# Twenty of 32 gated-conv projection tiles as ten seven-product pairs behind the SSD

## The chip, the cores and the metric

The kernel runs on one core of a Trainium2 chip. TensorE (PE) multiplies, VectorE (DVE), ScalarE (ACT) and GpSimd (POOL) work on tiles, SyncE (SP) issues the loads and stores. The metric is the device time of one execution in microseconds; less is better.

## The reference

Two layers of an encoder, 1024 tokens of width 1024, in float32. The change lies in the first, even layer: one input projection feeds a bidirectional Mamba-2 SSD (16 heads in 4 groups, chunks of 128 tokens) and a short gated convolution; both outputs go through one output projection.

```python
proj = x @ w_in
z, xbc, dt_raw, sc_bg, sc_cg, sc_h, sc_gate = _split(proj, EVEN_SIZES)
...
y_a = _rms_norm(y_a.reshape(b, S, SSD_INNER).astype(x.dtype) * jax.nn.silu(z), norm_g)
y_b = sc_bg * _depthwise_conv(sc_cg * sc_h, sc_conv_w, (1, 1)) * jax.nn.silu(sc_gate)
return jnp.concatenate([y_a, y_b], axis=-1) @ w_out
```

The four parts of the gated convolution (sc_bg, sc_cg, sc_h, sc_gate) are 1024 wide each: 32 tiles of 128 columns, which the kernel names `("br", q, j)`, q = 0 to 3 for the part and j = 0 to 7 for the tile. The second layer (latent attention and pooling) isn't touched.

## The kernel before

Each float32 operand is split into a high and a low half in the matmul's type (a cast on ScalarE gives the high one, a subtraction on VectorE or GpSimd the low one), and a product is three matmuls: high by high, high by low, low by high. A projection tile of 128 columns and 1024 tokens is eight steps (one for each 128 of the depth) of `mm6`, six matmuls of 512 columns; its PSUM tile is called `gps` in the traces, its weights come from `wraw` as `whi` and `wlo`, through the class `Weights`, which loads and splits them in the order in which the tiles are used.

`main_plan` writes the order of the even layer as a list of steps, and a queue of tile steps (`fm`) is pulled into it as filler. For each SSD group g it has two phases:

- p2, for each of eight chunks: the z tile (`op_z`, 24 matmuls of 256 columns, `zps`), the transposes of x and B (`xps`), the state products (`op_p2s`, `sps`). Then `op_p2b` runs the backward recursion over the chunks' states `hin`, on GpSimd (`hm`) and VectorE in turn.
- p3, for each of eight chunks: `op_p3f` makes the decay matrix: it loads rows `E` and `tb`, ScalarE takes their relu and `Dm`, VectorE their maximum, ScalarE the exp, VectorE multiplies by `Dm` and by the C-B product (`cbp`), and the result is split into `Mh` and `Ml`. `op_p3x` splits `hin` into `hh`, `hl` and x into `xs`. `op_p3b` multiplies them (`yo` from hh and hl, `yd` from Mh, Ml and xs), adds up in `ta` on GpSimd and VectorE, gates with z on GpSimd (`yg`), squares on ScalarE (`ta,ssq`) and stores the row to memory (`yad`).

The plan puts FB = 6 steps of filler ahead of p2, FC = 4 ahead of p3 and F3 = 7 into each p3 chunk. The filler is the 32 br tiles in the order of j; ahead of them go the X tiles of the next group (before p3) and its B and C tiles (behind p3). Behind the SSD, `op_ya` transposes the gated rows for the output projection (`yat`, `yas`, `ahi`, `alo`), with the last br tiles between; `ops` are the output projection's matmuls. A scheduler then orders each engine's instructions; every engine runs its own in that order.

Of the kernel before, what the change touches and what calls it, by code (L numbers as in the profile page):

```python
# [18 lines left out]
P = 128  # L19
# [44 lines left out]
F2, F3, FB, FT, FC = 0, 7, 6, 4, 4  # L64
ROPE_AT = (2, 2)
L1_ORDER = "t0 l2 t1 l3 t2 l4 t3 l5 m0 l6 m1 l7".split()
YB_AT = (0, 1, 3, 4, 6, 7, 9, 10)
X_AT = (10, 11, 12, 13)
WOB, WOI, WOG, PI, NV, LA = 2, 3, 1, 1, 0, 2
T4B, T2B, CVB, RAWB = 1, 10, 3, 2  # L70


def main_plan():
    ops = []
    queue = []

    def tile_steps(key):
        return [("fm", key, kk) for kk in range(KD)]

# [12 lines left out]
    pull(8)  # L92
    ops.append(("dt",))
    pull(len(queue))
    for j in range(8):
        for q in BR_ORDER:
            queue += tile_steps(("br", q, j))
    for g in range(G):
        ops.append(("z0", g))
        pull(FB)  # L100
        for c in range(NB):
            ops.append(("p2", g, c))
            ops.append(("z", g, c))
# [17 lines left out]
        if g + 1 < G:  # L121
            to_front([("B", g + 1), ("C", g + 1)])
            while any(s[1][0] in ("B", "C", "X") for s in queue):
                pull(1)
    ops.append(("end",))
    for c in range(NB):
        pull(FT)
        ops.append(("ya", c))
    pull(len(queue))
    return ops  # L130

# [16 lines left out]
def weight_index():  # L148
    idx = {}
    for key in weight_seq():  # L150
        idx.setdefault(key, len(idx))
# [73 lines left out]
class Weights:  # L225
    def __init__(self, k, pool, ahead=1):
        self.k, self.pool, self.ahead = k, pool, ahead
        self.seq, self.idx = weight_seq(), weight_index()
        self.loaded = self.done = self.used = 0
        self.raw, self.out = {}, {}  # L230

    def load(self, upto):
        while self.loaded < min(upto, len(self.seq)):
# [6 lines left out]
    def split(self, upto):  # L240
        nc = self.k.nc
        while self.done < min(upto, len(self.seq)):
# [9 lines left out]
            self.load(i + 2)  # L252

# [219 lines left out]
def layer0_main(k):  # L473
# [6 lines left out]
    sctx = ExitStack()  # L480
    k.dts_pool = sctx.enter_context(tc.tile_pool(name="dts", bufs=1))
    cvp = sctx.enter_context(tc.tile_pool(name="cvp", bufs=1))
# [4 lines left out]
    xhi = [view(big(k, f"xhi{h}"), KD) for h in range(2)]  # L487
    xlo = [view(big(k, f"xlo{h}"), KD) for h in range(2)]
# [3 lines left out]
    for kk in range(KD):  # L492
        raw = dtp.tile([P, 2, HALF], F32, name="xraw", tag="xraw", bufs=4)
# [5 lines left out]
        for h in range(2):  # L499
            split(nc, xhi[h][:, kk, :], xlo[h][:, kk, :], raw[:, h, :], V)  # L500
# [24 lines left out]
    def t4(name):  # L525
        return tp.tile([P, S], F32, name=name, tag="t4", bufs=T4B)
# [29 lines left out]

    def fm_finish(key, ps):
# [8 lines left out]
        elif kd in ("B", "C"):  # L566
# [6 lines left out]
            for h in range(2):  # L573
                sl = slice(HALF * h, HALF * h + HALF)
                v = conv_half(ps, 8 + 4 * q + g, st["xfm"][:, 2, sl] if q == 0 else None, h)
                split(nc, st["bc"][:, 2 * q, sl], st["bc"][:, 2 * q + 1, sl], v, V)
        else:
# [5 lines left out]
            elif q == 2:  # L583
                u = br["u"]
                V.tensor_tensor(out=u, in0=ps, in1=u, op=ALU.mult)
                w = lambda i: k.vec[:, V_SCW + 3 * j + i:V_SCW + 3 * j + i + 1]
                br["a"] = []
                for h in range(2):
                    acc = tp.tile([P, 512], F32, name="bra", tag="bra", bufs=2)
                    A.mul(out=acc, in_=u[:, hs[h]], mul=w(1))  # L590
                    for i, sh in ((0, -1), (2, 1)):
                        a0 = 1 if h == 0 and sh < 0 else 0
                        a1 = HALF - 1 if h == 1 and sh > 0 else HALF
                        lo = HALF * h + sh
                        V.scalar_tensor_tensor(out=acc[:, a0:a1], in0=u[:, lo + a0:lo + a1], scalar=w(i), in1=acc[:, a0:a1], op0=ALU.mult, op1=ALU.add)
                    br["a"].append(acc)
# [14 lines left out]
    def op_fm(key, kk):  # L611
# [4 lines left out]
        mm6(nc, halves(ps), wh[:, kk, :], wl[:, kk, :], [t[:, kk, :] for t in xhi], [t[:, kk, :] for t in xlo], kk == 0, kk == KD - 1)  # L616
# [11 lines left out]
    def op_z(g, c):  # L628
# [3 lines left out]
        for kk in range(KD):  # L632
            wh, wl = st["zw"][kk // 4]
            mm3(nc, ps, xhi[h][:, kk, o:o + P], xlo[h][:, kk, o:o + P], view(wh, 4)[:, kk % 4, :], view(wl, 4)[:, kk % 4, :], kk == 0, kk == KD - 1)
# [131 lines left out]
    def op_end():  # L766
# [6 lines left out]
        k.ahi = [view(big(k, f"ahi{h}"), KD) for h in range(2)]  # L773
        k.alo = [view(big(k, f"alo{h}"), KD) for h in range(2)]

    def op_ya(c):
        h, o = c // 4, (c % 4) * P
        for q in range(2):
            y = t2("yab")
            nc.sync.dma_start(out=y, in_=k.yad[c, :, HALF * q:HALF * q + HALF])  # L780
            V.tensor_scalar(out=y, in0=y, scalar1=k.rinv[:, c:c + 1], scalar2=None, op0=ALU.mult)
            ps = k.pb.tile([P, 512], F32, name="yat", tag="pb")
            for f in range(4):
                PE.transpose(out=ps[:, P * f:P * f + P], in_=y[:, P * f:P * f + P], identity=k.ident)
            t = cv("yas")
            V.tensor_tensor(out=view(t, 4), in0=view(ps, 4), in1=bc_last(k.vec[:, V_NG + 4 * q:V_NG + 4 * q + 4], P), op=ALU.mult)
            split(nc, k.ahi[h][:, 4 * q:4 * q + 4, o:o + P], k.alo[h][:, 4 * q:4 * q + 4, o:o + P], view(t, 4), V)

    table = {"fm": op_fm, "z0": op_z0, "z": op_z, "p2": op_p2, "p2s": op_p2s, "p2b": op_p2b, "p3f": op_p3f, "p3x": op_p3x, "p3b": op_p3b, "dt": op_dt, "rope": lambda: rope_tables(k, t2), "end": op_end, "ya": op_ya}
    for op in main_plan():  # L790
        table[op[0]](*op[1:])
    sctx.close()
# [25 lines left out]
def outproj0(k):  # L818
# [40 lines left out]
    for h in range(2):  # L859
# [529 lines left out]
```

## Time and profile before

| | us |
|---|---|
| median of 3 runs | 1444.57 (1444.01 to 1447.03) |
| profiled execution | 1445.73 |
| its span, first to last instruction | 1444.0 |
| PE busy | 1416.2 (98%) |
| DVE, ACT, POOL busy | 921.9, 749.1, 480.5 |
| granted TensorE clock, mean | 0.997 |

The SSD with its filler runs from about 65 to 729 us of the span, the output projection of the even layer follows, and the odd layer comes behind it. Busy time is the sum of an engine's instructions; the length of a matmul's row contains time in which the next one already runs, so the distance between starts is the price of one. A pair of starts of the same kind, say two `Mh`, shows the time that a chunk takes.

### The profile page before, as it was taken

To read this page: it belongs to the slowest core of one execution; us is meant where nothing else is said; L and a number is where in the kernel's file an instruction comes from. 1 tells how busy PE (TensorE), PEld (TensorE's weight loads), DVE (VectorE), ACT (ScalarE), POOL (GpSimd) and SP (SyncE) were. 2 spreads that over 40 slices of the span, in tenths; PEclk is the share of its full clock that TensorE was granted. 3 is DMA by queue.
4 is the path that set the end of the run, shared out by engine and by line. 5 is a ranking of instruction groups with operands and counts; after the bars stand their busy time and mean duration, and the time that the engine had idled before them with its cause. 6 is when DMAs were issued, how large, how long until landed. Compare 5 with 4: busy or idle time off the path is not lost.

```text
span 1444.0 us, 20351 instructions
## 1 busy us (share of the span) xinstructions
PE 1416.2 (98%) x7454; PEld 1208.9 (84%) x7454; DVE 921.9 (64%) x1608; ACT 749.1 (52%) x1567; POOL 480.5 (33%) x479
## 2 busy tenths in 40 slices
PE   7999999999999999999989999999999999999997
PEld 5898888888898888988868888898888888988886
DVE  5837666666687665647683543733326888888485
ACT  5447654576447773566443332522224788888510
POOL 0032541435322452445400160612320355556210
PEclk9999999999999999999999999999999999999999
DMA  6102331323203321133525556201110000001232
GB/s 219 48 30 89 113 84 38 93 78 111 70 30 103 112 86 52 59 110 95 164 99 175 204 175 200 89 31 59 44 37 1 1 1 1 1 30 59 89 117 88
DMA packets 46483, 118.57 MB, mean 82 GB/s; under 512 B 5808, under 2 KB 10288, under 8 KB 46384
## 3 DMA queue, kind: packets, MB, share of 16 engines
q1 hardware_dynamic: 46384, 117.27, 25.5%
q8 instruction: 59, 0.97, 0.3%
q14 instruction: 40, 0.33, 0.1%
HBM read 100.34 MB, written 16.91 MB: 81 GB/s over the span
## 4 chain that ended last, share of the span: by engine, by line
PE 44%; DVE 4%; issue 1%; ACT 1%; DMA 0%; POOL 0%; DVEq 0%; ACTq 0%; POOLq 0%
PE ops L377 4%; PE ops L378 4%; PE ops L380 4%; PE tps L1211 3%; PE fps L371 3%; PE fps L372 3%; PE fps L370 3%; PE o1ps L377 2%; PE o1ps L380 2%; PE o1ps L378 2%; PE yps L1226 2%; PE sps L370 2%; PE sps L372 2%; PE sps L371 2%; PE yps L1225 2%
## 5 line engine op out<-in xcount | busy, mean ns | idle before, releaser
L377 PE MATMUL gps<-xhi,whi 128*128 128x512 f32 x768 | 302.2, 394 | 0.0
L378 PE MATMUL gps<-xlo,whi 128*128 128x512 f32 x768 | 301.7, 393 | 0.0
L380 PE MATMUL gps<-xhi,wlo 128*128 128x512 f32 x768 | 242.6, 393 | 0.0
L249 DVE TENSOR_TENSOR wlo<-wraw,whi 128x1024 fp32r<-128x1024 f32 x100 | 137.5, 1377 | 109.4 <-ACT whi L248 99.5
L248 ACT CAST whi<-wraw 128x1024 fp32r<-128x1024 f32 x100 | 104.7, 1049 | 131.4 <-DMA wraw<-in_wt_dram 41.3
L377 PEld LDWEIGHTS gps<-xhi,whi 128*128 128x128 f32 x768 | 144.4, 188 | 29.0
L378 PEld LDWEIGHTS gps<-xlo,whi 128*128 128x128 f32 x768 | 144.4, 188 | 29.0
L380 PEld LDWEIGHTS gps<-xhi,wlo 128*128 128x128 f32 x768 | 142.9, 188 | 28.7
L1197 POOL TENSOR_SCALAR pt<-pt,sm 128x1024 f32<-128x1024 f32 x64 | 72.9, 1140 | 114.2 <-DVE sm L1196 63.3
L467 POOL TENSOR_TENSOR xdl<-xd,xdh 128x512 fp32r<-128x512 f32 (+1 forms) x32 | 36.9, 1153 | 206.5 <-ACT xdh L466 166.0
L467 DVE TENSOR_TENSOR PT<-tps,PT 128x512 fp32r<-128x512 f32 x128 | 84.1, 681 | 12.6 <-ACT PT L466 12.4
L1191 DVE TENSOR_REDUCE nm<-sps 128x1 f32<-128x1024 f32 x64 | 77.9, 1217 | 9.5 <-PE sps L372 9.2
L467 POOL TENSOR_TENSOR hl<-hin,hh 128x512 fp32r<-128x512 f32 (+1 forms) x32 | 38.7, 1210 | 135.4 <-ACT hh L466 135.4
L814 POOL TENSOR_TENSOR rs<-rs,neghalf 128x1 f32<-128x1 f32 x16 | 12.9, 808 | 209.4 <-DMA wraw<-in_wt_dram 81.4
L1195 ACT ACTIVATE pt<-sps,nm 128x1024 f32<-128x1024 f32 x64 | 71.8, 1122 | 17.4 <-DVE nm L1192 13.1
L466 ACT CAST PT<-tps 128x512 fp32r<-128x512 f32 x128 | 69.9, 588 | 16.2 <-PE tps L1211 15.6
L370 PE MATMUL fps<-x1hi,whi 128*128 128x512 f32 x192 | 74.9, 390 | 0.0
L372 PE MATMUL fps<-x1hi,wlo 128*128 128x512 f32 x192 | 74.8, 389 | 0.0
L371 PE MATMUL fps<-x1lo,whi 128*128 128x512 f32 x192 | 74.7, 389 | 0.0
L370 PE MATMUL zps<-whi,xhi 128*128 128x256 f32 x256 | 73.9, 289 | 0.0
L372 PE MATMUL zps<-whi,xlo 128*128 128x256 f32 x256 | 72.4, 283 | 0.0
L371 PE MATMUL zps<-wlo,xhi 128*128 128x256 f32 x256 | 72.3, 282 | 0.0
(338 smaller groups left out, 3597.1 us busy)
## 6 DMA issues: line engine op xcount, KB each, us to landing
wraw<-in_wt_dram SPq DMA_DIRECT2D x100, 512.0 KB, 3.6
E<-crow SPq DMA_DIRECT2D x32, 256.0 KB, 3.9
tb<-crow SPq DMA_DIRECT2D x32, 256.0 KB, 4.4
yad<-yg SPq DMA_DIRECT2D x32, 128.0 KB, 1.7
ybd<-bra SPq DMA_DIRECT2D x16, 256.0 KB, 2.2
yab<-yad SPq DMA_DIRECT2D x16, 256.0 KB, 3.7
ybr<-ybd SPq DMA_DIRECT2D x8, 512.0 KB, 4.2
h<-in_x_dram SPq DMA_DIRECT2D x8, 512.0 KB, 5.4
```

What stands on the lines that cost most here:

```text
L248: nc.scalar.copy(out=hi, in_=raw)
L249: nc.vector.tensor_tensor(out=lo, in0=raw, in1=hi.bitcast(F32), op=ALU.subtract)
L370: nc.tensor.matmul(out, shi, mhi, start=start, stop=False)
L371: nc.tensor.matmul(out, shi, mlo, start=False, stop=False)
L372: nc.tensor.matmul(out, slo, mhi, start=False, stop=stop)
L377: nc.tensor.matmul(out, shi, mhi, start=start, stop=False)
L378: nc.tensor.matmul(out, shi, mlo, start=False, stop=False)
L380: nc.tensor.matmul(out, slo, mhi, start=False, stop=stop)
L467: lo_eng.tensor_tensor(out=lo, in0=src, in1=hi.bitcast(F32), op=ALU.subtract)
L1191: V.tensor_reduce(out=nm, in_=ps, axis=AX.X, op=ALU.max)
L1195: A.activation(out=pt, in_=ps, func=AF.Exp, bias=nm, scale=ATT_SCALE, accum_out=sm)
L1197: GP.tensor_scalar(out=pt, in0=pt, scalar1=sm, scalar2=1.0, op0=ALU.mult, op1=ALU.mult)
```

## The change

The plan keeps the br tiles of j = 0 to 2 (12 tiles) as filler, with F3 = 4 and FC = 6. The 20 tiles of j = 3 to 7 become ten pairs, (1, j) with (2, j) and (3, j) with (0, j), in a stage behind the SSD. A pair is a product of a 2x2 block matrix of weights (two tiles by two halves of the depth) and a 2x2 block matrix of x (two halves of the depth by two halves of the tokens), made by seven block products instead of eight: `op_sp` runs one product of four depth steps by three matmuls of 512 columns, 84 matmuls for a pair where two tiles had 96. The sums that the scheme needs of x are made once, `op_tp(0)` to `op_tp(3)`, two of them in the chunks of g = 3 and two behind it; those of the weights are made for each pair by `op_sw`. `snap` copies a product out of PSUM and `comb` adds the next one to it.

Other parts of the change: the B and C tiles of the next group are put ahead of p3 along with the X tiles; `RAWB` raises the raw weight buffers from 2 to 4, and the raw x tiles at the start and those of `op_tp` use them too; x lies in four tiles of high and low halves; `Weights` holds the output projection's weights back until the last pair; `op_ya` works on a 1024-wide row at once, its scaling goes to ScalarE, two of its eight calls stand in the pair stage and six behind it.

```diff
-F2, F3, FB, FT, FC = 0, 7, 6, 4, 4
+F2, F3, FB, FC = 0, 4, 6, 6
+J0 = 3
...
-T4B, T2B, CVB, RAWB = 1, 10, 3, 2
+T4B, T2B, CVB, RAWB = 1, 10, 3, 4
...
-    for j in range(8):
+    for j in range(J0):
         for q in BR_ORDER:
             queue += tile_steps(("br", q, j))
...
-            to_front([("X", 2 * g + 2), ("X", 2 * g + 3)])
+            to_front([("X", 2 * g + 2), ("X", 2 * g + 3), ("B", g + 1), ("C", g + 1)])
...
+            if g == G - 1 and c == 2:
+                ops.append(("tp", 0))
+            if g == G - 1 and c == NB - 1:
+                ops.append(("tp", 1))
             pull(F3)
             ops.append(("p3b", g, c))
...
     ops.append(("end",))
-    for c in range(NB):
-        pull(FT)
+    ops.append(("tp", 2))
+    pull(4)
+    ops.append(("tp", 3))
+    pull(4)
+    ops += [("sw", 0, i) for i in range(SW_N)]
+    pull(len(queue))
+    ops.append(("sw", 1, 0))
+    for n in range(NP):
+        for i in range(7):
+            ops.append(("sp", n, i))
+            if n + 1 < NP and 0 < i + 1 < SW_N:
+                ops.append(("sw", n + 1, i + 1))
...
+PAIRS = [p for j in range(J0, 8) for p in ((("br", 1, j), ("br", 2, j)), (("br", 3, j), ("br", 0, j)))]
...
+    def op_tp(kk):
+        ra, rb = (W.pool.tile([P, 1024], F32, name="xtraw", tag="wraw", bufs=RAWB) for _ in range(2))
...
+        for o, p, q in ((a0, a1, a0), (a1, b1, a1), (b1, b1, a0), (b0, b0, b1)):
+            V.tensor_tensor(out=o, in0=p, in1=q, op=ALU.subtract)
+        t = big(k, "xT4").rearrange("p (s a t) -> p s a t", s=2, a=4)
+        for i, r in ((0, ra), (2, rb)):
+            split(nc, t[:, 0, i:i + 2, :], t[:, 1, i:i + 2, :], view(r, 2), V)
...
+    def op_sw(n, i):
+        st = sp[n]
+        if i == 0:
...
+                r = W.pool.tile([P, 1024], F32, name="sraw", tag="wraw", bufs=RAWB)
+                nc.sync.dma_start(out=r, in_=a["wt"][W.idx[key]])
...
+    PRODS = (("L11", 0, "A"), ("L12", 1, "B"), ("S2", "T2", "A"), ("S3", "T3", "D"), ("S1", "T1", "A"), ("L22", "T4", "D"), ("S4", 3, "A"))
...
+        for kk in range(4):
...
+            for m, (s_, x_) in enumerate(((wh, mh), (wh, ml), (wl, mh))):
+                PE.matmul(ps, s_[:, kk, :], x_, start=fresh and kk == 0 and m == 0, stop=kk == 3 and m == 2, skip_group_check=True)
```

The order of PE within the p3 chunks of g = 3, before, at one chunk's yo and yd:

```order
L377 MATMUL gps<-xhi_92,whi 128x512
L378 MATMUL gps<-xlo_94,whi 128x512
L380 MATMUL gps<-xhi_91,wlo 128x512
L380 MATMUL gps<-xhi_92,wlo 128x512
L377 MATMUL gps<-xhi_91,whi 128x512
L378 MATMUL gps<-xlo_93,whi 128x512
L371 MATMUL yo<-hl,bc 128x512
L372 MATMUL yo<-hh,bc 128x512
L377 MATMUL gps<-xhi_92,whi 128x512
L752 MATMUL yd<-xs,Mh 128x128
```

And after the change, at the end of one chunk and the start of the next:

```order
2655 L789 MATMUL yd<-xs,Ml 128x64
2656 L788 MATMUL yd<-xs,Mh 128x128
2657 L789 MATMUL yd<-xs,Ml 128x64
2658 L735 MATMUL cbp<-bc 128x256
2659 L736 MATMUL cbp<-bc 128x128
2660 L398 MATMUL yo<-hh,bc 128x512
2661 L399 MATMUL yo<-hl,bc 128x512
2662 L400 MATMUL yo<-hh,bc 128x512
2663 L788 MATMUL yd<-xs,Mh 128x128
```

The gps matmuls that stood between a chunk's own ones are not there any more in this stage.

The order of ACT in a p3 chunk of g = 3, before (brt is a br tile's work, whi a weight's split):

```order
477 L248 CAST whi<-wraw 128x1024
478 L763 ACTIVATE ta,ssq<-yg 128x256
479 L713 ACTIVATE E<-E 128x512
480 L716 COPY tb<-cbp 128x128
481 L603 ACTIVATE brt<-gps 128x512 x2
482 L466 CAST Mh<-E 128x512
483 L466 CAST hh<-hin 128x512
484 L466 CAST xs<-zx 128x4x64
485 L711 ACTIVATE Dm<-consts,dtb,dtd 128x128 x4
```

And after:

```order
554 L746 ACTIVATE tb<-tb,cs 128x128 x4
555 L799 ACTIVATE ta,ssq<-yg 128x256
556 L749 ACTIVATE E<-E 128x512
557 L752 COPY tb<-cbp 128x128
558 L494 CAST Mh<-E 128x512
559 L494 CAST hh<-hin 128x512
560 L494 CAST xs<-zx 128x4x64
561 L747 ACTIVATE Dm<-consts,dtb,dtd 128x128 x4
```

The chunk's own operations keep their order, and what stood between them for the tiles is gone.

The order of SP after the change, around the row loads of the first chunks of g = 3 (xtraw are the raw tiles of `op_tp`):

```order
109 L800 DMA yad<-yg 128x256 x2
110 L817 DMA xtraw<-in_xT_dram 128x2x512 x2
111 L739 DMA E<-crow 128x512
112 L740 DMA tb<-crow 128x512
113 L817 DMA xtraw<-in_xT_dram 128x2x512 x4
114 L739 DMA E<-crow 128x512
115 L740 DMA tb<-crow 128x512
```

Six of the eight raw x tiles stand between the row loads, four of them ahead of those of the second chunk.

## Rows read from the trace of the kernel before

**Rows 1.** Busy time by stretch: length, then each engine's busy us, clock, DMA.

```profile
640.00:720.00 80.00, 80.00 (x390) 67.11 (x390) 51.99 (x84) 46.06 (x116) 41.78 (x41) 1.00 0.41 124
```

**Rows 2.** Busy time by stretch behind the SSD, same columns.

```profile
731.00:740.00 9.00, 5.55 (x34) 3.88 (x31) 9.00 (x16) 4.82 (x9) 0.08 (x1) 1.00 0.18 58
740.00:750.00 10.00, 8.90 (x36) 7.13 (x37) 9.64 (x15) 4.74 (x9) 2.86 (x2) 0.83 0.45 154
```

**Rows 3.** Timeline of PE, g = 0: start, length, what.

```profile
201.17 0.62 PE L380 MATMUL gps<-xhi,wlo 128*128 128x512 f32 x2
...
202.53 0.61 PE L380 MATMUL gps<-xhi,wlo 128*128 128x512 f32 x2
...
218.44 0.22 PE L752 MATMUL yd<-xs,Mh 128*128 128x128 f32 x1
...
219.25 0.48 PE L380 MATMUL gps<-xhi,wlo 128*128 128x512 f32 x1
```

**Rows 4.** Busy time of the gps matmuls alone, g = 3: PE busy (count), clock, DMA.

```profile
602.00:624.00 22.00, 21.46 (x92) 1.00 0.38 120
624.00:706.00 82.00, 73.67 (x303) 1.00 0.36 107
```

**Rows 5.** Timeline of ACT, DVE and POOL in one chunk of g = 3.

```profile
665.75 0.62 ACT L466 CAST Mh<-E 128x512 fp32r<-128x512 f32 x1 [1.86 <-DVE E L719]
...
668.05 1.65 ACT L711 ACTIVATE Dm<-consts,dtb,dtd 128x128 f32<-128x128 f32 x4
...
668.81 2.12 DVE L249 TENSOR_TENSOR wlo<-wraw,whi 128x1024 fp32r<-128x1024 f32 x1
...
669.79 1.73 POOL L467 TENSOR_TENSOR xs<-zx,xs 128x256 fp32r<-128x256 f32 x1
670.78 1.28 ACT L710 ACTIVATE tb<-tb,cs 128x128 f32<-128x128 f32 x4
671.48 0.73 POOL L757 TENSOR_TENSOR ta<-to,ta 128x256 f32<-128x256 f32 x1
672.25 0.42 DVE L759 TENSOR_TENSOR ta<-yd,ta 128x256 f32<-128x256 f32 x1 [1.32 <-POOL ta L757]
672.71 0.42 DVE L760 TENSOR_TENSOR ta<-yd,ta 128x256 f32<-128x256 f32 x1
...
673.26 1.05 POOL L762 TENSOR_TENSOR yg<-ta,zx 128x256 f32<-128x256 f32 x1 [1.05 <-issue]
...
674.35 0.42 ACT L763 ACTIVATE ta<-yg 128x256 f32<-128x256 f32 x1 [2.29 <-POOL yg L762]
...
674.77 0.62 ACT L713 ACTIVATE E<-E 128x512 f32<-128x512 f32 x1
...
675.42 0.69 DVE L714 TENSOR_TENSOR E<-E,Dm 128x512 f32<-128x512 f32 x1 [1.69 <-ACT E L713]
...
677.40 0.62 ACT L466 CAST Mh<-E 128x512 fp32r<-128x512 f32 x1 [1.86 <-DVE E L719]
677.92 0.62 ACT L466 CAST hh<-hin 128x512 fp32r<-128x512 f32 x1
...
678.62 1.29 POOL L467 TENSOR_TENSOR hl<-hin,hh 128x512 fp32r<-128x512 f32 x1 [3.73 <-ACT hh L466]
...
679.86 0.74 POOL L467 TENSOR_TENSOR xs<-zx,xs 128x256 fp32r<-128x256 f32 x1
```

**Rows 6.** DMA issues of the page: KB, median us from issue to landing.

```profile
tb<-crow SPq DMA_DIRECT2D x32, 256.0 KB, 4.4
```

**Rows 7.** Timeline of PE, DVE and ACT at the start of g = 1's chunks.

```profile
270.78 0.28 PE L372 MATMUL zps<-whi,xlo 128*128 128x256 f32 x1
...
287.80 0.42 DVE L691 TENSOR_TENSOR hin<-hin,hm 128x256 f32<-128x256 f32 x1
...
289.18 0.39 ACT L466 CAST hh<-hin 128x256 fp32r<-128x256 f32 x1
```

**Rows 8.** One line's instructions, L249: count, min/median/max ns, first and last.

```profile
L249 DVE TENSOR_TENSOR wlo<-wraw,whi x100: 1201/1225/3375, 14.5 to 1062.5; 128x1024 fp32r<-128x1024 f32 x100
```

More of the change, by code (lines that the diff above doesn't have):

```diff
@@ L241, in split @@
         nc = self.k.nc
-        while self.done < min(upto, len(self.seq)):
+        while self.done < min(upto, self.limit):
             i = self.done
@@ L252, in split, with release @@
             self.load(i + 2)
+    def release(self):
+        self.limit = len(self.seq)
+        self.split(self.used + 1 + self.ahead)
     def get(self, key):
@@ L499, in layer0_main @@
         for h in range(2):
-            split(nc, xhi[h][:, kk, :], xlo[h][:, kk, :], raw[:, h, :], V)
+            split(nc, *xhl(h, kk), raw[:, h, :], V)
         if kk == 1:
@@ L555, in layer0_main, with br_conv @@
     br = {}
+    def br_conv(u, j):
+        hs = [slice(0, HALF), slice(HALF, S)]
+        w = lambda i: k.vec[:, V_SCW + 3 * j + i:V_SCW + 3 * j + i + 1]
+        br["a"] = []
+        for h in range(2):
+            acc = cvp.tile([P, 512], F32, name="bra", tag="bra", bufs=2)
+            A.mul(out=acc, in_=u[:, hs[h]], mul=w(1))
+            for i, sh in ((0, -1), (2, 1)):
+                a0 = 1 if h == 0 and sh < 0 else 0
+                a1 = HALF - 1 if h == 1 and sh > 0 else HALF
+                lo = HALF * h + sh
+                V.scalar_tensor_tensor(out=acc[:, a0:a1], in0=u[:, lo + a0:lo + a1], scalar=w(i), in1=acc[:, a0:a1], op0=ALU.mult, op1=ALU.add)
+            br["a"].append(acc)
     def fm_finish(key, ps):
@@ L585, in fm_finish @@
                 V.tensor_tensor(out=u, in0=ps, in1=u, op=ALU.mult)
[L586 to L596, printed above, removed]
+                br_conv(u, j)
             elif q == 0:
@@ L615, in op_fm @@
         wh, wl = view(whi, KD), view(wlo, KD)
-        mm6(nc, halves(ps), wh[:, kk, :], wl[:, kk, :], [t[:, kk, :] for t in xhi], [t[:, kk, :] for t in xlo], kk == 0, kk == KD - 1)
+        mm6(nc, halves(ps), wh[:, kk, :], wl[:, kk, :], *zip(*(xhl(h, kk) for h in range(2))), kk == 0, kk == KD - 1)
         if kk == KD - 1:
@@ new lines, in snap, with comb, silu2, gate @@
+    def snap(ps):
+        t = k.w2.tile([P, HALF], F32, name="snap", tag="snap", bufs=3)
+        A.copy(out=t, in_=ps)
+        return t
+    def comb(out, ps, t):
+        V.tensor_tensor(out=out, in0=ps, in1=t, op=ALU.add)
+    def silu2(h, src):
+        th = cv("brt")
+        A.activation(out=th, in_=src, func=AF.Tanh, scale=0.5)
+        V.scalar_tensor_tensor(out=th, in0=th, scalar=1.0, in1=src, op0=ALU.add, op1=ALU.mult)
+        br["th", h] = th
+    def gate(h, j):
+        acc = br["a"][h]
+        GP.tensor_tensor(out=acc, in0=acc, in1=br.pop(("th", h)), op=ALU.mult)
+        nc.sync.dma_start(out=k.ybd[j, :, HALF * h:HALF * h + HALF], in_=acc)
@@ new lines, in layer0_main @@
+    k.ay = {}
+    def op_ya(c):
+        if c // 2 not in k.ay:
+            k.ay[c // 2] = big(k, f"ay{c // 2}").rearrange("p (s a t) -> p s a t", s=2, a=KD)
+        o = (c % 2) * P
+        t = k.ay[c // 2]
+        y = W.pool.tile([P, S], F32, name="yab", tag="wraw", bufs=RAWB)
+        nc.sync.dma_start(out=y, in_=k.yad[c])
+        A.mul(out=y, in_=y, mul=k.rinv[:, c:c + 1])
+        ps = k.pa.tile([P, 1024], F32, name="yat", tag="pa")
+        for f in range(KD):
+            PE.transpose(out=ps[:, P * f:P * f + P], in_=y[:, P * f:P * f + P], identity=k.ident)
+        V.tensor_tensor(out=view(y, KD), in0=view(ps, KD), in1=bc_last(k.vec[:, V_NG:V_NG + KD], P), op=ALU.mult)
+        split(nc, t[:, 0, :, o:o + P], t[:, 1, :, o:o + P], view(y, KD), V)
```

169 lines of the change are left out of this document (128 added, 41 removed).

## The prediction

> **What bounds the kernel now.** I read the busy time by stretch first, then the PE rows themselves, then the other engines' rows in one SSD chunk. In the last group's chunk stage PE is busy for all of 80 us, while VectorE has 52, ScalarE 46 and GpSimd 42 [rows 1]. The only gap of any size in the part that the change touches is behind the SSD: between 731 and 750 us PE is busy 14.5 of 19 us, and the clock granted in the second half is 0.83 [rows 2]. So before the change the SSD costs TensorE time and nothing else. A row's length is no price there, since matmuls overlap: from 201.17 to 202.53 us six matmuls of 512 columns start, which makes 0.2267 us each [rows 3], though each row shows 0.39.
>
> What keeps PE full is the filler. In the g = 3 chunk stage 303 of the matmuls are gps ones, 73.7 of 82 us; between the last z product and the first yd of the same group 92 more, 21.5 of 22 [rows 4]. A chunk's own matmuls are few: eight yd in 0.81 us (218.44 to 219.25) [rows 3], and by the same pitch three yo of 512 columns in 0.68 and two cbp in 0.18, so 1.7 us.
>
> Without filler a chunk goes at the pace of a loop that runs through three engines, since ScalarE's order puts the square of chunk c (ta, ssq) ahead of the exp of chunk c+1. I walked it in [rows 5], start to start: Mh to hh 0.52 (677.40, 677.92), to hl on GpSimd 0.70 (678.62), to xs 1.24 (679.86), to ta 0.74 (the length of xs), ta on GpSimd to the first ta on VectorE 0.77 (671.48, 672.25), to the second 0.46 (672.71), to yg 0.55 (673.26), to the square 1.09 (674.35), to exp 0.42 (674.77), to E*Dm 0.65 (675.42), to the next Mh 1.98 (677.40). Sum **9.1 us**. The same loop as it ran, with a weight split and a conv in it, took 11.65 (Mh at 665.75 and 677.40).
>
> **The sum, part by part**, from the profiled execution's own 1445.7 us, which lies 1.2 above the median.
>
> *Fewer products.* Twenty tiles of 48 matmuls become ten pairs of 84: 960 - 840 = 120 matmuls at 0.2267 us, **-27.2 us**, if PE stays as full as it is.
>
> *The filler is gone.* In the changed order 12 gated-conv tiles are left for the SSD, and they don't reach. I count gps matmuls between one chunk's yd and the next one's: g = 0 has what it had (32 to 68); g = 1 has 38, 47, 18, 48, 48, 0, 0; g = 2 has 44, 42, 20, 48, 44, 48, 40; g = 3 has seven times 0, where before no such piece had under 34. A piece takes the longer of its PE work and the loop. For a bare loop I take 9.5 us: bounds 8.4 (ScalarE's own operations of a chunk: Dm and E 2.7, from 668.05 to 670.78, tb 1.3, the square 0.4, exp 0.6, Mh and hh 0.5 each, two short copies an estimated 0.5, some 6.5 together, plus the 1.9 that it waits for VectorE ahead of Mh [rows 5]) and the observed 11.65; the walk is the nearest, and I add 0.4 for meetings that a walk doesn't show.
> - g = 3: the first piece is longer. SyncE now has four xtraw loads ahead of the E and tb loads of chunk 1, and those wait for buffers that open only after the T1 split on ScalarE. A row load takes 4.4 us [rows 6], then come relu, max, exp and the products up to Mh (670.78 to 677.40, 6.6 us, of which the square's wait falls away). I take 14.5 us (bounds 9.5 and 18). With six pieces of 9.5 that is 71.5 us, with 7 x 1.7 = 12 us of PE work: **59 us idle**.
> - g = 1: two bare pieces, 2 x (9.5 - 1.7), and one with 18 matmuls, 9.5 - 5.8: **19**.
> - g = 2: one piece with 20, 9.5 - 6.2: **3**.
> - From the last z product to the first yd of g = 1 and g = 2 there were 96 and 88 gps, now 41 and 42, some 12 us of PE work with the state products. The chain there is the backward recursion: last z product at 270.78, last hin at 287.80, hh at 289.18 [rows 7], 18 us, of which the convolutions of the filler take a part. I take 18 to the first yd (bounds 12 and 23.5, as before): **12** for both. In g = 3 there are 77 and no gap.
>
> Together **+93** (bounds some 60 and 130).
>
> *Into the pair stage.* The first pair's weights load into buffers that the raw tiles of T2 and T3 hold until the last x split behind g = 3; then come the load and the two halves of a split (a 1024-wide wlo takes VectorE 1.2 us alone [rows 8]). **+8**, bounds 3 and 15.
>
> *The pair stage.* 84 x 0.2267 = 19.0 us of PE for each pair. VectorE has three 1024-wide splits and about ten 512-wide operations of 0.68 each, about 11 us; ScalarE's and GpSimd's share, in operations of the lengths of [rows 5], I estimate at 7 and 9. PE bounds it. A product of bank A waits for the copy of an earlier one, but another bank's twelve matmuls (2.7 us) lie between. **+4** for the ten, bounds 0 and 12.
>
> *The clock.* After the gaps of 731 to 740 us the stretch of 10 us behind them was granted 0.83 [rows 2], so 1.7 us were lost. PE comes back to dense work behind a long gap about once at full price, **+2** (0 to 6).
>
> *Behind the pairs.* Two of the eight ya tiles are done within the stage, and the others come in one 1024-wide piece each; of the 4.5 us of gap in [rows 2] and what else is lost by 760 us I take **-4** (-8 to +4). The raw x tiles share four weight buffers at the start: **+1** (-1 to +4).
>
> Sum: 1445.7 - 27.2 + 93 + 8 + 4 + 2 - 4 + 1 = 1522.5; against the median, 1.2 lower: **1521 us**.
>
> **Weighed beside it.** At 669.79 GpSimd's xs took 1.73 us while VectorE split a wlo in 2.12; at 679.86, with no split beside it, 0.74 [rows 5]. The Trainium skill, "SBUF — State Buffer", section "Who interferes with whom", says that a VectorE instruction with two SBUF inputs and a GpSimd instruction that reads SBUF lock each other out of a shared port for a whole instruction, which these rows agree with. By that rule a bare chunk, which has no splits, runs nearer the walk than the observed loop: with 9.1 the sum is 1517, with 11.65 it is 1542.
>
> **Rivals.**
> - *Everything still fits under PE* (the other side). The pair products or the remaining tiles cover the chunks, and the 27.2 us are gained: 1417 with the tail's gain. The smaller terms add 11 us, so it is no loss as long as PE's idle time stays under 16; with 12 us of own work in the seven bare pieces of g = 3 that is (12 + 16) / 7 = 4 us a piece, even if g = 1 and g = 2 lost nothing. ScalarE alone has some 6.5 us of work in one, and the order has no pair product ahead of the last yd of g = 3. 0.03.
> - *Half of the stalls are hidden.* Loop at the bound of 8.4, recursion hidden (12 us to yd), the transition at 3: 1521 - 10 - 12 - 5 - 4 = 1490. For it speaks that fewer fillers mean fewer meetings. 0.18.
> - *The loop doesn't get shorter without fillers.* 11.65 a piece, the recursion as long as before, stalls in the pair stage: 1521 + 21 + 11 = 1553, with more in the pairs 1560. For it: what was in the observed loop, a split and a conv, lay partly in the loop's own waits, so taking it out may save less than the walk says. 0.2.
> - *The clock stays low in the bare chunks.* The granted clock of 0.83 behind gaps of 2 us [rows 2] makes it likely that it falls to 1.2 GHz in a stage where PE works 1.7 of 9.5 us. Then yd takes 1.6 instead of 0.8 us, within the loop between xs and the first ta; GpSimd's ta (0.77) hides half: +0.8 on nine pieces, 1528. The Trainium skill, "TensorE: Matmul & The Clock Gate", section "HAM oscillation — how this bites in real kernels", tells of a kernel whose bursts between waits all run at the lower clock; no run here shows it yet. 0.2, inside the forecast's own range.
>
> **How the numbers follow.** The forecast with its clock variant, 1505 to 1540, holds 0.55; the short case 0.18, the long one 0.2, faster 0.03, and 0.04 is for a stage that is slower for a reason that I don't see (pair stage not bound by PE: at 24 us a pair it would be 1570). Range 1488 to 1558. A measurement of this kernel can tell 0.2%, about 3 us, from no change. Faster 0.03, same 0.02, slower 0.95: the loss from g = 3 alone, even at the least pace that ScalarE's own work allows (7 x 6.5 - 12 = 33 us), is above the 27 of the gain.
>
> **What would show it.** In the changed profile the g = 3 chunk stage has PE busy under 2 in 10 for some 70 us, with waits of yd and yo for Mh, xs and hh; Mh follows Mh every 9 to 10 us; two pieces at the end of g = 1 look the same; the pair stage is full of PE at 19 to 19.5 us a pair. It is wrong if Mh follows Mh in under 5 us, or if the pairs take over 21 us each.

## The result: 1543.7 us, and the profile after

The changed kernel takes **1543.69 us** (four runs, 1541.95 to 1544.82), the kernel before beside it 1444.64: a ratio of **1.0681 [1.0663, 1.07]**. Slower was forecast, with 1521 (1488 to 1558): the time lies 22.7 above the forecast and inside the range. The profiled execution took 1544.03 us with a span of 1541.8, so all that follows accounts for 97.8 us of span.

The page first. These are the totals of PE, and of the view in 40 slices (38.5 us each) the rows of PE and of its clock:

```profile
PE 1424.7 (92%) x7334; PEld 1204.4 (78%) x7334; DVE 989.2 (64%) x1660; ACT 792.0 (51%) x1620; POOL 539.9 (35%) x514
PE   7999997979799954699999999999999999999997
PEclk9999998989899965799999999999999999999999
```

PE was 98% busy before. Now there are three holes of 2 to 3 us in 10 in slices 7, 9 and 11 (from 231, 308 and 385 us), and a deep one in slices 15 to 17, with the clock down to 0.5 beside it. From slice 18 on PE is full. The busy time by stretch (length, then PE, PEld, DVE, ACT, POOL with their counts, granted clock, DMA share and GB/s) puts them in their stages:

```profile
340.00:350.00 10.00, 4.07 (x17) 3.45 (x16) 6.27 (x12) 5.85 (x16) 5.37 (x7) 0.50 0.04 14
385.00:398.00 13.00, 2.58 (x10) 1.47 (x8) 11.27 (x21) 10.30 (x25) 3.81 (x5) 0.70 0.40 122
555.00:627.00 72.00, 31.15 (x99) 23.72 (x99) 37.40 (x69) 48.49 (x136) 36.54 (x43) 0.50 0.28 72
700.00:750.00 50.00, 50.00 (x222) 41.44 (x221) 35.50 (x39) 19.12 (x27) 18.35 (x11) 1.00 0.27 84
```

The third row is the chunk stage of g = 3, which answers to [rows 1]: 99 matmuls where 80 us of before had 390. The fourth is the pair stage: PE alone is full there. The first is the end of g = 1's bare chunks, the second the start of g = 2's chunk stage, with 10 matmuls in 13 us. What PE waited for (total, times, longest), over the whole program:

```profile
PE yo L398 <- ACT hh L494: 48.3, 11, 6.8
PE gps L405 <- DVE cacc L579: 14.2, 2, 7.2
PE yo L399 <- POOL hl L495: 5.0, 9, 0.7
PE sA L900 <- ACT whi L494: 4.5, 1, 4.5
```

The first and third are the bare chunks, the second the starts of g = 1's and g = 2's chunk stages, the fourth the step into the pairs.

To put a number on each stage I took the distance between the starts of successive matmuls less the price of the first at full clock (0.2267 us for 512 columns, the shorter ones in proportion or a little above), and summed it by stage. It counts idle time and the loss to a low clock together. Before it is 13 us from the first yd to the last; after:

| stage | forecast, us | measured |
|---|---|---|
| 120 matmuls fewer | -27.2 | -27.2 |
| start | +1 | +1 |
| g = 1: last z product to first yd | 12 with g = 2's | 12.0 |
| g = 1 chunks | 19 | 18.4 |
| g = 2 z stage | 0 | 6.6 |
| g = 2: last z product to first yd | (above) | 14.7 |
| g = 2 chunks | 3 | 7.8 |
| g = 3: last z product to first yd | 0 | 6.3 |
| g = 3 chunks, first to last yd | 59 | 59.6 |
| the rest of the SSD, less the 13 of before | 0 | -8 |
| step into the pairs and their first 19 us | +8, clock +2 | 12.0 |
| pair stage from 650 us | +4 | 2.6 |
| behind the last product | -4 | -8.4 |
| sum | 76.8 | 97.4 |

The rows are rounded (the spans differ by 97.8), and with the short matmuls priced a little otherwise a row moves by up to 1.5 us. Some 2.7 us in each z stage and 1.7 in each stage of chunks were lost before too; the row for the rest of the SSD takes them back. The SSD gives +117.4 where 93 was forecast, 24 more, of which the other rows give back 4: that is why the time lies above the forecast.

### The profile page after: what moved, and what is told of

It reads as the page before. It is cut to its first block, busy times and chain, and to the rows that moved or that the text cites. A ratio compares the mean times of both kernels' runs of the same rounds, so it can differ in the third digit from the quotient of the medians.

```text
span 1541.8 us, 20340 instructions
## 1 busy us (share of the span) xinstructions
PE 1424.7 (92%) x7334; PEld 1204.4 (78%) x7334; DVE 989.2 (64%) x1660; ACT 792.0 (51%) x1620; POOL 539.9 (35%) x514
## 4 chain that ended last, share of the span: by engine, by line
PE 53%; DVE 3%; ACT 1%; issue 1%; DMA 0%; DVEq 0%; ACTq 0%; SPq 0%
PE sA L900 6%; PE ops L405 3%; PE ops L408 3%; PE ops L406 3%; PE sD L900 3%; PE tps L1384 3%; PE fps L400 3%; PE fps L399 3%; PE fps L398 3%; PE yps L1399 2%; PE o1ps L408 2%; PE o1ps L405 2%; PE o1ps L406 2%; PE sps L398 2%; PE sps L400 2%; PE sps L399 2%
## 5 line engine op out<-in xcount | busy, mean ns | idle before, releaser
L405 PE MATMUL gps<-x,whi 128*128 128x512 f32 x448 | 180.0, 402 | 17.5 <-DVE cacc L579 14.2
L406 PE MATMUL gps<-x,whi 128*128 128x512 f32 x448 | 177.7, 397 | 0.0
L273 DVE TENSOR_TENSOR wlo<-wraw,whi 128x1024 fp32r<-128x1024 f32 x80 | 108.9, 1362 | 101.9 <-ACT whi L272 91.7
L272 ACT CAST whi<-wraw 128x1024 fp32r<-128x1024 f32 x80 | 83.9, 1049 | 133.9 <-PE ops L408 64.5
L408 PE MATMUL gps<-x,wlo 128*128 128x512 f32 x448 | 142.2, 397 | 1.3 <-DVE wlo L273 1.0
L405 PEld LDWEIGHTS gps<-x,whi 128*128 128x128 f32 x448 | 85.4, 191 | 37.5 <-issue 14.5
L408 PEld LDWEIGHTS gps<-x,wlo 128*128 128x128 f32 x448 | 83.8, 190 | 21.2 <-DVE wlo L273 4.4
L406 PEld LDWEIGHTS gps<-x,whi 128*128 128x128 f32 x448 | 85.5, 191 | 16.9
L1368 ACT ACTIVATE pt<-sps,nm 128x1024 f32<-128x1024 f32 x64 | 71.8, 1123 | 17.4 <-DVE nm L1365 13.1
L398 PE MATMUL zps<-whi,x 128*128 128x256 f32 x256 | 74.5, 291 | 2.7 <-DVE xd L699 1.4
L400 PE MATMUL zps<-whi,x 128*128 128x256 f32 x256 | 72.7, 284 | 0.0
L399 PE MATMUL zps<-wlo,x 128*128 128x256 f32 x256 | 72.7, 284 | 0.0
```

The costliest lines, as they stand in the source:

```text
L272: nc.scalar.copy(out=hi, in_=raw)
L273: nc.vector.tensor_tensor(out=lo, in0=raw, in1=hi.bitcast(F32), op=ALU.subtract)
L398: nc.tensor.matmul(out, shi, mhi, start=start, stop=False)
L399: nc.tensor.matmul(out, shi, mlo, start=False, stop=False)
L400: nc.tensor.matmul(out, slo, mhi, start=False, stop=stop)
L405: nc.tensor.matmul(out, shi, mhi, start=start, stop=False)
```

## What sets the pace of a bare chunk

One chunk of g = 3, in order of time; columns are start, length, engine, line, operation, and in brackets the engine's idle time before it with what ended it:

```profile
592.32 0.62 ACT L494 CAST Mh<-E 128x512 fp32r<-128x512 f32 x1 [1.86 <-DVE E L755]
592.84 0.61 ACT L494 CAST hh<-hin 128x512 fp32r<-128x512 f32 x1
593.51 0.80 PE L398 MATMUL yo<-hh,bc 128*128 128x512 f32 x1 [4.64 <-ACT hh L494]
593.53 1.27 POOL L495 TENSOR_TENSOR hl<-hin,hh 128x512 fp32r<-128x512 f32 x1 [3.71 <-ACT hh L494]
594.76 0.73 POOL L495 TENSOR_TENSOR xs<-zx,xs 128x256 fp32r<-128x256 f32 x1
595.45 1.54 POOL L793 TENSOR_TENSOR ta<-to,ta 128x256 f32<-128x256 f32 x2
597.02 0.42 DVE L795 TENSOR_TENSOR ta<-yd,ta 128x256 f32<-128x256 f32 x1 [2.76 <-POOL ta L793]
598.03 1.05 POOL L798 TENSOR_TENSOR yg<-ta,zx 128x256 f32<-128x256 f32 x1 [1.05 <-issue]
599.12 0.42 ACT L799 ACTIVATE ta<-yg 128x256 f32<-128x256 f32 x1 [1.46 <-POOL yg L798]
599.53 0.61 ACT L749 ACTIVATE E<-E 128x512 f32<-128x512 f32 x1
600.17 0.69 DVE L750 TENSOR_TENSOR E<-E,Dm 128x512 f32<-128x512 f32 x1 [1.68 <-ACT E L749]
602.15 0.62 ACT L494 CAST Mh<-E 128x512 fp32r<-128x512 f32 x1 [1.86 <-DVE E L755]
```

The loop is the one that was walked in [rows 5], and every link in it waits for the one before: PE 4.64 us for hh, GpSimd 3.71 for hh, VectorE 2.76 for GpSimd's ta, ScalarE 1.46 for yg. No engine is full, ScalarE (48 of 72 us) least idle. Mh to Mh is 9.83 us, and five such pieces in a row are between 9.8 and 9.9.

The walk said 9.1. One link holds the difference: GpSimd's two additions `ta` now stand together behind xs (1.54, x2), and from their start to VectorE's ta it is 1.57 us, where the walk had 0.77. In the chunk of before one of the two ran earlier (the row at 671.48 in [rows 5] is an x1). So the engine's order, not a slower operation, made the loop longer. One reading in the forecast was a chunk off: the square of chunk c stands ahead of the exp of chunk c+2, since chunk c+1's Mh is made already; the path and its times are the same. So two chunks lie side by side in the loop: hh, hl and xs are those of chunk c+1, while ta, yg and the square belong to chunk c. The `ta` at 597.02 is the fourth of the group and adds the fourth yd, which had started at 586.05. Several links are therefore an engine's order and not data: GpSimd's ta of chunk c stands behind hl and xs of chunk c+1.

## The experiments

Each is an edit of the changed kernel, but the one where the text says so. A time without a range is that of a single execution. All are compared with 1543.7 us for the changed kernel and 1443.3 to 1445.3 for the kernel before, beside which they ran.

**The loop itself.** The square of chunk c goes behind the exp, so that the exp doesn't wait for yg (it is written one chunk later, and the small tiles, ta and yg among them, get six buffers instead of four):

```diff
-        return tp.tile([P, 256], dt, name=name, tag="t1", bufs=4)
+        return tp.tile([P, 256], dt, name=name, tag="t1", bufs=6)
...
-        A.activation(out=ta, in_=yg, func=AF.Square, accum_out=k.ssq[:, c, g:g + 1])
+        with k.tc.issue_after(st["x", min(c + 2, NB - 1)]):
+            A.activation(out=ta, in_=yg, func=AF.Square, accum_out=k.ssq[:, c, g:g + 1])
```

> The changed kernel with one ScalarE operation in another place: the square of chunk c is issued behind the exp of chunk c+2 and not ahead of it. Theory 'a bare chunk goes at the pace of a loop through ScalarE, GpSimd and VectorE': exp no longer waits for yg and the square, about 1.0 us off each of ten bare pieces: Mh to Mh from 9.8 to 8.8 us in g = 3, and 1534 to 1537 us in all. Rival 'the lower clock of PE, or the row loads, set the pace': 9.8 us as before and 1543 us.

It took **1536.50 us**, 7.2 less, and Mh follows Mh every 9.2 us (8.8 was expected):

```profile
593.64 0.63 ACT L749 ACTIVATE E<-E 128x512 f32<-128x512 f32 x1 [0.88 <-DVE E L748]
594.33 0.42 ACT L776 ACTIVATE ta<-yg 128x256 f32<-128x256 f32 x1
596.60 0.62 ACT L494 CAST Mh<-E 128x512 fp32r<-128x512 f32 x1 [1.76 <-DVE E L755]
605.78 0.62 ACT L494 CAST Mh<-E 128x512 fp32r<-128x512 f32 x1 [1.77 <-DVE E L755]
```

The exp now waits 0.88 for VectorE's maximum instead of 1.46 for yg: taking out one link shows that the loop is the pace, and that the next path is only 0.6 us shorter. Of the 7.2 us 3.3 lie in the chunks of g = 3, most of the others ahead of them. The two extra buffers weren't run alone.

**Is PE's own work on the loop?** 126 matmuls of 512 columns whose result nobody reads, 18 in each chunk of g = 3 but the last:

```diff
+        if g == G - 1 and c < NB - 1:
+            pad = k.pb.tile([P, 512], F32, name="pad", tag="pb")
+            for i in range(18):
+                PE.matmul(pad, bc[:, 2, blk], bc[:, 3, 0:512], start=True, stop=True)
```

> The changed kernel with 18 more matmuls of 512 columns behind the yd of each of seven chunks of g = 3, into a PSUM tile that nobody reads: 126 x 0.2267 = 28.6 us of PE work. Theory 'PE is idle there and the loop sets the pace': the work goes into the idle time, the clock of the stage goes up from 0.5, and the time stays within 3 us of 1543.7. Rival 'PE's time counts there': 1572 us. Rival 'the low clock costs much': 1535 us or less.

**1543.46 us**: 28.6 us of PE work at full clock (126 x 0.2267) cost nothing. The stretch, and below it the pads alone:

```profile
555.00:627.00 72.00, 55.76 (x216) 42.88 (x215) 39.24 (x70) 46.83 (x130) 34.63 (x40) 0.83 0.30 70
...
555.00:627.00 72.00, 39.70 (x126) 29.76 (x126) 0.83 0.30 70
```

Mh to Mh stays at 9.8 to 9.9. The clock rises from 0.50 to 0.83 and the time doesn't change, so the low clock of the bare chunks isn't what they wait for either. PE's time is free here; the change has carried away the work that could use it.

**Is the scheme to blame?** The 20 tiles stay behind the SSD, but as plain tiles of 48 matmuls, without block sums (in this run the tiles come in the order of parts 1, 2, 3, 0, so that the multiplication by part 0 isn't in the output):

```diff
     for n in range(NP):
-        for i in range(7):
-            ops.append(("sp", n, i))
...
+        for key in PAIRS[n]:
+            queue += tile_steps(key)
...
+        pull(len(queue))
```

> The changed kernel with the same SSD and the same filler, but the 20 tiles of the stage behind it as plain tiles of 48 matmuls (no products by the block scheme, no sums of x or of weights); they are held behind the last yd. Theory 'the SSD has lost its filler' (the scheme itself is sound and worth its 120 matmuls): PE has 27 us more in the stage; against that the raw x tiles and their sums leave the start of g = 3 (some 13 us there) and the step into the stage (some 3): 1555 us, 1548 to 1566. Rival 'the scheme costs what it saves' (waits for copies out of PSUM, sums of weights): 1540 us or less.

**1559.93 us**, 16.2 more. Its gps matmuls behind the SSD, 960 of them:

```profile
610.00:850.00 240.00, 221.10 (x960) 181.91 (x960) 19.41 (x25) 10.96 (x15) 0.97 0.18 60
```

They run from 618 to 842 us, 224 in all. So the seven-product scheme does what it says: less work by 27 us. The SSD without the sums ends 8 us earlier (last yd at 617.9 instead of 626.1), which gives part of it back. What loses is the place. The 20 tiles are 218 us of PE work at 0.2267 each, which the SSD's chunks had hidden their own loop behind; without them the SSD idles for some 118 us more, and the work at its new place hides nothing.

**The starts of the chunk stages.** The first theory was that convolutions of the B and C tiles, now ahead of p3, hold up the backward recursion on VectorE. For g = 1 to 3 three of their four taps are left out, which also leaves those terms out of the output:

```diff
-        for j, sh in ((1, -1), (0, -2), (3, 1)):
+        for j, sh in ((1, -1), (0, -2), (3, 1)) if idx < 8 or (idx - 8) % 4 == 0 else ():
```

> The changed kernel without three of the four convolution taps in the B and C tiles of g = 1 to 3 (left out of the computation: 12 VectorE operations of about 0.73 us for each pair of tiles, 8.8 us for each group). Theory 'the X, B and C tiles that the change puts side by side ahead of p3 fill VectorE just where the backward recursion needs it': from the last z product to the first yd, 22.9 us in g = 1 and 26.0 in g = 2 in the changed kernel, goes to 18 to 20, and the time to 1532 to 1539 us. Rival 'there PE waits for weights or buffers, or its own work sets the time': 22 us or more stay and 1541 us or more.

**1543.50 us**, and the wait of 7.2 us stands in it as it did:

```profile
PE gps L405 <- DVE cacc L579: 14.2, 2, 7.2
```

The theory fell: hh comes 17.4 us (g = 1) and 19.6 us (g = 2) behind the last z product, where it came 17.6 and 19.9 us behind it, so these taps don't hold the recursion. The first yd does come earlier, after 20.4 and 24.9 us instead of 22.9 and 26.0, but only because fewer gps stand ahead of it in PE's order; what PE loses in the two stretches is the same within 1 us (11.4 and 14.8 us, before 12.1 and 14.9). What holds the gps is then an X tile's convolution, whose taps ran here as before. In the changed kernel, around the first chunk of g = 2:

```profile
393.72 0.78 ACT L575 ACTIVATE cacc<-gps,vec 128x512 f32<-128x512 f32 x1
394.38 0.37 ACT L718 COPY hin<-sps 128x256 f32<-128x256 f32 x1
398.23 0.77 PE L405 MATMUL gps<-x,whi 128*128 128x512 f32 x1 [6.98 <-DVE cacc L579]
403.48 0.59 PE L405 MATMUL gps<-x,whi 128*128 128x512 f32 x1
404.78 0.39 ACT L494 CAST hh<-hin 128x256 fp32r<-128x256 f32 x1
409.85 0.28 PE L398 MATMUL yo<-hh,bc 128*128 128x256 f32 x1
410.89 0.22 PE L788 MATMUL yd<-xs,Mh 128*128 128x128 f32 x1
```

The last z product of g = 2 ends at 384.9. hh comes 20 us later, but yo another 5 later, because the gps ahead of it in PE's order could start only at 398.23, when the convolution had read the tile's PSUM, and ran at a granted clock of 0.50 till 403.5. That this is the X tiles' convolution, with the copies behind it in ScalarE's order, is read from the rows; a run without their taps wasn't made.

**The sums in g = 3.** In the changed kernel SP's xtraw issues hold up the row loads, so that ScalarE waits for a row, and the sums stand between VectorE's steps of the recursion:

```profile
536.43 1.28 ACT L746 ACTIVATE E<-E,cs 128x128 f32<-128x128 f32 x4 [2.74 <-DMA E<-crow]
```

Writing all of the sums behind the SSD:

```diff
-            if g == G - 1 and c == 2:
-                ops.append(("tp", 0))
-            if g == G - 1 and c == NB - 1:
-                ops.append(("tp", 1))
...
-    ops.append(("tp", 2))
+    ops += [("tp", 0), ("tp", 1), ("tp", 2)]
```

> The changed kernel with all four sums of x made behind the SSD, none in the chunks of g = 3. Theory 'the sums stand in the way at the start of g = 3, through VectorE and through SyncE's queue': from the last z product to the first yd 25.4 us goes to 18 to 20, the first Mh to the second from 17.3 to some 11, 12 us won; against that the step from the last yd to the first product grows from 6 us to some 16 to 18: 1540 to 1546 us in all. Rival 'they cost nothing there': g = 3 as it was and 1554 us.

It took **1542.38 us**, inside the expected range, but told nothing apart: the scheduler drew the sums back to where they had been, with the xtraw subtractions at 534 to 556 us. The next run holds them behind the last chunk's exp, last ta and last store:

```diff
+        with tc.issue_after(k.end[0]), tc.issue_after(k.end[1]), tc.issue_after(k.end[2]):
+            make_t(kk)
```

> As the run with the sums of x behind the SSD, but now held there on SyncE, VectorE and ScalarE, behind the last chunk's own work (in that run the scheduler had drawn them ahead into g = 3 again). Theory 'the sums stand in the way at the start of g = 3': from the last z product to the first yd 25.4 us goes to 18 to 21, the first Mh to the second from 17.3 to some 11; the step from the last yd to the first product grows from 6 us to some 15: 1539 to 1546 us. Rival 'they cost nothing there': g = 3 as it was and 1552 us or more.

**1555.81 us**, 12 more. From the last z product to the first yd of g = 3 it is now 19.2 us instead of 25.4, so the sums do cost 6 us there, and 2 more in the first piece (Mh to Mh 15.5 instead of 17.3). But they were done in idle time, and behind the last chunk they stand alone:

```profile
PE sA L900 <- ACT whi L490: 30.6, 1, 30.6
```

PE waits 30.6 us there, where the changed kernel waits 4.5. The theory was right on the start of g = 3 and wrong on the step, which was expected at some 15 us and takes 31.

**Fewer pairs, spread filler.** If a chunk's loop is 9.8 us, it carries (9.8 - 1.7) / 0.2267 = 36 gps for nothing, so the pairs could be fewer and the filler spread evenly. Three runs tried it, with six pairs and 42 gps held to each chunk, six pairs with 36 and more slack, and four pairs (24 tiles of filler). Of the first:

```diff
-J0 = 3
+J0 = 5
+FBG, FCG, F3G = (0, 0, 0, 0), (8, 8, 8, 8), (7, 7, 7, 7)
...
+        with k.tc.issue_after(k.anchor) if k.anchor is not None else ExitStack():
+            mm6(nc, halves(ps), wh[:, kk, :], wl[:, kk, :], *zip(*(xhl(h, kk) for h in range(2))), kk == 0, kk == KD - 1)
```

> Filler given back and spread: tiles of j = 0 to 4 stay as filler (20 instead of 12), six pairs instead of ten, each filler step is kept behind the yd of the chunk ahead of it so that all chunks get 42 of its matmuls, X, B and C tiles follow the first br ones, all sums of x behind the SSD. Theory 'only the lost filler costs': PE full through the SSD, 72 matmuls saved (16 us), some 8 lost on the way into the stage and 9 won behind it: 1430 us, 1422 to 1445. Rival 'the stage of pairs costs': six tenths of the loss stay, 1500 us.

> Six pairs, 20 tiles as filler. Each filler step may go one chunk ahead of its place in the plan, not more: 36 matmuls in each chunk of all four groups, 6 steps at each z stage, one sum of x in g = 3, three behind it with 8 steps of filler between them. Theory 'time is lost where PE finds no filler: in the chunks, at the z stage, at the step into the pairs': chunks at about 11 us, z stages back to 34 to 36, the step 10 us, 1441 us (1432 to 1456). Rival 'the chunk's loop with filler in it is slower than 11 us': 1460 us and more.

> Four pairs, 24 tiles as filler, placed as in the run with six pairs but 42 to 48 matmuls in each chunk. Theory: PE has work all through the SSD, 48 matmuls saved (11 us), 10 lost at the step into the pairs, some 8 won behind them, some 5 of small gaps: 1442 us (1434 to 1452). Rival: the pair stage or its entry costs more for each pair than it saves, 1455 us or more.

They took **1490.87**, **1523.22** and **1478.18 us**: better than ten pairs, far from the 1430 to 1442 expected, and none as good as no pair at all; in all three the rival came nearer than the theory. In the first the z stages, left without filler, wait for the last chunk of the group before. By the sum of the table the four of them lose some 33 us (before 11), the chunks 27 (before 7) and the step into the pairs 18 (before 2):

```profile
PE zps L395 <- DVE ta L797: 9.9, 3, 3.3
PE sA L901 <- ACT whi L491: 6.5, 1, 6.5
PE yd L789 <- DVE to L785: 4.8, 7, 1.7
```

In the second, chunks with 36 gps take 10 to 17 us, 12.5 on average and not 9.8. With filler, its splits and evictions lie among the loop's own operations; that this is the reason is argued, no run separates it. The bare pace must not be taken as the pace of a chunk that is partly filled. In the third the queue is empty two chunks before the end: from 640 to 700 us

```profile
640.00:700.00 60.00, 35.31 (x132) 26.99 (x132) 42.90 (x56) 31.15 (x66) 32.48 (x29) 0.72 0.38 108
```

The smallest step back is two pairs with the filler and the order of before:

```diff
-F2, F3, FB, FC = 0, 4, 6, 6
-J0 = 3
+F2, F3, FB, FC = 0, 7, 6, 4
+J0 = 7
```

> Two pairs instead of ten: 28 tiles stay as filler with the numbers of the kernel before (7 steps in a chunk, 6 and 4 ahead), B and C behind p3 as before, the four tiles of j = 7 as two pairs behind the SSD, the ya steps in and behind them. 24 matmuls (5.4 us) less. In the order only the last three chunks of g = 3 are short of filler (6, 0, 0 matmuls). Theory 'a pair costs what its tiles' filler was worth': about 20 us of idle PE in those chunks and 6 at the step into the stage, against 5.4 of products, 20 of plain tiles that stood behind the last yd before, and some 8 behind the pairs: 1450 us, 1444 to 1458. Rival 'a few pairs pay': 1438 us or less.

**1477.34 us** (1476.89 to 1478.32), 1.022 [1.0203, 1.0237] of the kernel before, and 27 above what was expected. The 24 matmuls saved are 5.4 us. The last gps ends at 679.4, so the chunks behind it are bare:

```profile
660.00:740.00 80.00, 51.89 (x209) 40.97 (x208) 54.41 (x77) 45.84 (x103) 40.55 (x39) 0.74 0.31 98
```

By the same sum as in the table it loses 34 us from 650 to the last yd (711), where before lost 2, and 6.5 in the step (before 1). The expectation had 20 us for those chunks. Before, the tiles of j = 7 had covered just these chunks and the start of `op_ya`.

**The other parts of the change without pairs.** `op_ya` by whole rows with its scaling on ScalarE, four raw buffers, x in four tiles; all 32 tiles as filler again:

```diff
-F2, F3, FB, FC = 0, 4, 6, 6
-J0 = 3
+F2, F3, FB, FC, FT = 0, 7, 6, 4, 4
+J0 = 8
```

> The changed kernel's other edits without its pairs: all 32 tiles as plain filler with the numbers of the kernel before (7 steps in a chunk, 6 and 4 ahead), B and C behind p3 as before, no sums, no stage; what stays is the new tiles of x, four raw weight buffers shared with the raw x, the new ya. Theory 'the loss is the filler's alone': the SSD as in the kernel before, 0 to 8 us won behind it, 1 lost at the start: 1436 to 1445 us. Rival 'the other edits cost as well': 1450 us or more.

**1459.87 us** (1459.28 to 1462.61), 1.0105 [1.0088, 1.0122]: 15 us slower than the kernel before, so the rival held. The SSD runs as before (last yd stage from 703.2 us, before 704.6); the loss is behind it, in the transposes of `op_ya`:

```profile
PE yat L936 <- ACT yab L933: 10.5, 1, 10.5
```

The new `op_ya` loads, scales and transposes a whole row, and nothing covers the first one. In the changed kernel the pair stage does.

**The saving at its old place.** From the kernel before, one depth step in eight of the 20 tiles left out, 120 matmuls, with nothing moved (so those tiles miss that part of the sum):

```diff
+        last = KD - 2 if key[0] == "br" and key[2] >= 3 else KD - 1
+        if kk <= last:
```

> The kernel before with six matmuls (the last step of depth) left out of each of the 20 tiles of j = 3 to 7, so 120 matmuls or 27.2 us of PE less, all else in its place: what the scheme's saving would be worth if the tiles could stay the SSD's filler. Theory 'PE alone bounds the SSD with its filler': 1416 us, 1413 to 1420. Rival 'the chunk's loop with filler in it takes about 11 to 12 us, as long as PE, so that less PE work gives less': 1424 to 1440 us.

**1436.50 us**, in the rival's range: of the 27.2 only some 8 reach the end. Not for the rival's reason alone, though: the last gps ends at 699.3 instead of 728.8, so PE is through with the filler earlier by the whole saving, while the last yd comes only 5 us earlier (700.2 instead of 705.4). Then:

```profile
690.00:740.00 50.00, 33.24 (x168) 27.14 (x167) 38.79 (x73) 18.55 (x38) 12.59 (x13) 0.86 0.45 145
```

PE is idle for 17 of these 50 us: the tiles that had covered the first rows of `op_ya` are done before those rows are there (`yat` waits 9.1 us for `yab`). Where work is a cover, saving it shows only up to the next thing that it had covered.

## Why the prediction was right, and where it was off

*What bounds before, and the filler's role*: right. PE idle in g = 3's chunks was forecast at 59 us and measured at 59.6, that in g = 1's at 19 and 18.4. That the sums agree so closely is in part luck. In g = 3 the pieces from yd to yd are 11.9, 8.4, four times 9.8 and 9.0 us, where 14.5 and six times 9.5 were taken. In g = 1 the piece with 18 gps takes 6.0 us and the two bare ones 7.0 and 9.0, where 9.5 each was taken; most of what is missing there PE lost in the pieces with filler ahead of them. A sign came out otherwise too: PE was to be busy under 2 in 10, and the row shows 31.15 of 72 us, since it adds up row lengths, which are longer at the lower clock; at full price the eight chunks of 1.7 us are some 13. The pairs, forecast at 19 to 19.5 us, follow each other every 19.04 us from the fourth on. The rows that decide it are [rows 4], the count of gps that leave, and the walk of [rows 5].

*From the last z product to the first yd*: the step that failed. 18 us were taken by [rows 7], less than the 23.5 of before because some filler leaves. It measured 22.9, 26.0 and 25.4 in g = 1, 2 and 3. The 18 is the distance to hh (18.4 in [rows 7]), and hh did come 17.6 us behind the last z product in g = 1; between hh and yd lie hl, yo and what stands ahead of them in PE's order. That link is 5.3 us in g = 1 and 6.1 in g = 2, and it had been 5.4 in the kernel before (289.18 to 294.62): the term stopped one link short. In a bare chunk the link takes 3.0 us (592.84 to 595.88); the other 2 to 3 are, by the rows, gps ahead of yo that had waited 7 us for a convolution. In g = 3, where "no gap" was forecast, the sums make the stretch 6 us longer, which the held run shows. The two terms were 15 us too small in g = 1 and 2 and 6 in g = 3. hh itself comes 2.3 us later in g = 2 than in g = 1. The delay is there already at VectorE's xd of the last chunk (385.22 in g = 2, 249.94 in g = 1, so 2.2 us later against the last z product), and PE's last state products wait for its split; why xd is late stays open.

*The z stage and the chunks of g = 2*: another 6.6 and 4.8 that the forecast didn't have. After g = 1's bare chunks PE starts g = 2's z stage at a clock of 0.50 (the row of 340 to 350 us); it is back at 1.00 by 354 us and costs some 1.5 us there. More goes to two waits for VectorE behind that, 0.9 us for the last bare chunk's ta and 1.4 for xd. In the chunks, by the rows, yo and yd wait 2.0 us for their own operands, in the piece with 20 gps and the one behind it, and two gps 1.1 us for a weight's split, where the clock is at 1.00. No run tests this. The forecast let the bare chunks end where their loop ends, and not where the full stage behind them has what it needs.

*Step, clock and pairs*: +14 forecast, 14.6 measured. The pair stage is bound by PE, 50.00 of 50 us, as forecast. *Behind the pairs*: -8.4 against -4, since the row pieces of `op_ya` wait for nothing there; the run without pairs shows that this gain is the pair stage's cover and not the edit's own.

*The rivals*: "everything fits under PE" would need pieces of 4 us; they are 9.8. "Half hidden" wants 8.4 and fell too. "The loop doesn't get shorter" wants 11.65: the bare loop is shorter than that, but the recursion was indeed as long as before, which that rival held and the forecast didn't. "The clock stays low" is true in the rows, 0.50 over 72 us; it was priced at 0.8 a piece by way of yd, and costs nothing in the bare chunks, since VectorE's ta waits for GpSimd's (2.76 us) and not for yd: the yd that it adds had started 11 us earlier, so yd isn't on the loop, and the run with the pads bears that out.

## What to carry to other kernels

Before work is moved off a full engine, ask what runs beside it: the filler's price in a stage is its time less what the stage would idle without it. Here 218 us of it left some 118 us of idle time behind, so it had cost 100 us at its old place; as pairs it costs 190 (840 x 0.2267) at the new one. Walk the bare stage's loop link by link in the order in which each engine will run it; a pace so found held within 0.7 us of 9.8, but it is the pace of an empty chunk alone, and half filled chunks don't follow it. For the start of a stage measure to the instruction that the next stage needs (here yd), not to the last operation of the chain that seems to set it.

## What the runs showed of the hardware

A granted clock of 0.50, the 1.2 GHz level, over the whole chunk stage of g = 3, with PE busy for 31 of 72 us, and no change of the time when 126 more matmuls raised it to 0.83. The price was paid where dense work came next: the first 13 matmuls of 512 columns of g = 2's chunk stage start 0.43 us apart until 403.5 us and 0.23 after that, and the first pair's likewise until 636 us, about 2.5 us each time.
